# Block products for the MLP's first matrix, with weight sums added in a DRAM scratch

## The chip, the cores and the metric

The kernel runs on one core of a Trainium2 chip. The metric is the device time of one execution in microseconds. The core has five engines that run side by side, each through its own list of instructions in order: PE (matrix products, with a weight load for each), DVE and ACT (element by element), POOL (the slower general engine) and SP (which issues transfers). SP, ACT and POOL can issue transfers; 16 DMA engines carry them. An instruction waits on semaphores that other engines or finished transfers raise, and while it waits, everything behind it on its engine waits too.

## The reference

Two layers over one sequence of 512 tokens and 1024 features, in float32. Each layer is a mixer (attention and mLSTM) and an MLP:

```
def hybrid_layer(x, ...):
    h = rmsnorm(x, norm_mix)
    z = h @ w_in                      # 1024 x 4360: q, k, v, mLSTM q, k, v, gates
    ... att = sliding_window_attention(q_a, k_a, v_a, att_sinks)
    ... hm = mlstm_chunkwise(q_m, k_m, v_m, i_pre, f_pre)
    mixed = sigmoid(g_a) * (att @ w_att_branch) + sigmoid(g_m) * (hm @ w_m_branch)
    x = x + mixed @ w_out
    u = relu(rmsnorm(x, norm_ffn) @ w_ff1)      # 1024 x 4096
    return x + (u * u) @ w_ff2                  # 4096 x 1024
```

The attention looks at its own block of 128 queries and the block before it (window 128).

## The kernel before, in words

**Precision.** Every large product is made of three: each operand is split into a high part in the matrix unit's fast format (ACT copies it, `wh`, `uh`, `i`) and the rest (DVE subtracts, `wl`, `ul`, `i`), and `mm3` (L207) issues high x high, high x low and low x high into the same PSUM bank. One matmul has a 128x128 stationary block and up to 512 moving columns. So each weight element is loaded by SP, split by ACT and DVE, and used by PE.

**The mixer** (`mixer`, L359) computes the projections in groups of 12 matmuls per loaded 128x512 block of weights (`chunk`, L164: three raw buffers and four split ones). `weave` (L251) lays the dense groups out as steps of a quarter unit each and drops side work between them at given places: the attention's transposes, scores, softmax and outputs, and the mLSTM. POOL has small parts of that side work: the squares of q for its norm (L466) and of k (L469), the rotary products (L492 to L497), and the masks of the attention's probabilities (L593, L595: two for the block's own keys and two for the block before, per block b of queries and kv head, from the second block on). The attention's output matmuls (L45, `aux<-t,v`) need those masked tiles, and the branch product `att @ w_att_branch` (`mm<-a,wh`) needs the outputs.

**The MLP** (`mlp`, L802) goes through the 4096 hidden units in four parts of 1024. The first matrix is done plainly (`First`, L853): per part four groups of 256 units, each 8 x 2 x 3 = 48 matmuls of 512 columns (the 512 tokens move). Its result is scaled by the token's norm along the columns (`rowf`, made by `along`, L310), made non-negative and squared. The second matrix is done per part as one step of a 2x2 block product with seven block products in place of eight (Strassen in Winograd's form; `slots_of`, L925): the halves of the tokens and of the part's hidden units on one side, the halves of the hidden units and of the 1024 output columns on the other. Each block product has two half slots of 12 matmuls of 512 columns. The sums of weight blocks that it needs are made by DVE in SBUF (`w_minus`, L829, 128x1024, eight per part), those of the hidden units too (`u_op`, L833). The first matrix's slots of the next part stand between the second's slots of this part, and a half slot's weights are split up to five half slots ahead (`prepare`).

**What sets the order.** The program is written as Python code, and a scheduler then orders the instructions of each engine: each goes to the earliest place at which its model of the chip has the operands and the engine ready, in order of priority (what is written earlier, or under `high_priority`, first). An instruction without operands that are still being made can so move far ahead of the place where it was written. Transfers are told apart by 8 completion semaphores for those of SP and ACT (DMAHW0 to 7) and 8 for those of POOL (DMASW0 to 7), used in turn; a transfer waits at its issue until the one before it on its semaphore is complete.

The seven products' order in the kernel before, as its code has it:

```
            p1 = product("x", True, w1, lambda: a11, [(0, 0, False)])
            p5 = product("y", True, w5, s1, [(1, 1, False)])
            ...
            f = [first_slot(part + 1, q, nxt) for q in range(4)]
            return [p1, f[0], p5, p6, f[1], p3, p7, f[2], p2, f[3], p4]
```

## Time and profile before

| | |
|---|---|
| time, median of 3 runs | 1337.35 us (1336.09 to 1338.18) |
| the profiled execution, first to last instruction | 1335.6 us |
| instructions | 16885 |
| layer 0: mixer, then MLP (by the trace's stages) | 0 to 340 us, 340 to 662 us |
| layer 1: mixer, then MLP | 662 to 1000 us, 1000 to 1335 us |
| PE, DVE, ACT, POOL busy | 98%, 69%, 50%, 8% |
| bytes moved by DMA | 125.02 MB, mean 94 GB/s |

The profile gives no time for the profiled execution beside its span; the median of the runs lies 1.75 us above that span. Each engine's busy time is a share of the whole span, so an engine can be the limit in one stage and idle in another: the stages are read with the table of windows. A busy PE says that matmuls follow each other, not how fast: they overlap, so what one costs is the distance between starts, not the "mean ns" of its row. The chain that ended last tells which engine was waited for, at each place, by the work that set the end.

### The profile page before, as it was taken

To read this page: it belongs to the slowest core of one execution; us is meant where nothing else is said; L and a number is where in the kernel's file an instruction comes from. 1 tells how busy PE (TensorE), PEld (TensorE's weight loads), DVE (VectorE), ACT (ScalarE), POOL (GpSimd) and SP (SyncE) were. 2 spreads that over 40 slices of the span, in tenths; PEclk is the share of its full clock that TensorE was granted. 3 is DMA by queue.
4 is the path that set the end of the run, shared out by engine and by line. 5 is a ranking of instruction groups with operands and counts; after the bars stand their busy time and mean duration, and the time that the engine had idled before them with its cause. 6 is when DMAs were issued, how large, how long until landed. Compare 5 with 4: busy or idle time off the path is not lost.

```text
span 1335.6 us, 16885 instructions
## 1 busy us (share of the span) xinstructions
PE 1312.4 (98%) x6106; PEld 1078.1 (81%) x6106; DVE 926.3 (69%) x1409; ACT 666.4 (50%) x1201; POOL 106.7 (8%) x215
## 2 busy tenths in 40 slices
PE   8999999999999999999999999999999999999998
PEld 6877788888788888888888777888887888888886
DVE  4688764474576876868947887554646778678687
ACT  5458765544334344343554687554434444344343
POOL 4512310000000000000015013000000000000000
PEclk9999999999999999999999999999999999999999
DMA  5322122421523133131024221243216242322211
GB/s 151 108 72 72 56 79 74 140 95 64 189 95 126 63 127 125 64 119 46 34 65 123 67 71 64 72 122 96 99 54 207 73 132 81 125 95 95 95 48 63
DMA packets 87282, 125.02 MB, mean 94 GB/s; under 512 B 8216, under 2 KB 45184, under 8 KB 87200
## 3 DMA queue, kind: packets, MB, share of 16 engines
q1 hardware_dynamic: 86240, 123.30, 29.3%
q8 instruction: 48, 0.79, 0.2%
q10 hardware_dynamic: 576, 0.53, 0.1%
q0 software_dynamic: 384, 0.13, 0.1%
q14 instruction: 34, 0.28, 0.1%
HBM read 121.84 MB, written 2.10 MB: 93 GB/s over the span
## 4 chain that ended last, share of the span: by engine, by line
PE 88%; DVE 6%; ACT 4%; issue 1%; DMA 1%; POOL 0%; ACTq 0%; SPq 0%; DVEq 0%; POOLq 0%
PE mm L45 82%; PE aux L45 4%; PE aux L49 2%; ACT t L574 1%; DVE wl L191 1%; ACT wh L190 1%; DVE t L561 1%; DVE t L611 0%; DMA w<-in_w_in_dram 0%; DVE t L201 0%; ACT wh L825 0%; DVE t L538 0%; ACT junk L287 0%; DVE t L579 0%; DMA grow<-in_norm_mix_dram 0%
## 5 line engine op out<-in xcount | busy, mean ns | idle before, releaser
L45 PE MATMUL mm<-i,wh 128*128 128x512 f32 x1664 | 522.6, 393 | 2.1 <-DVE a L661 1.2
L45 PEld LDWEIGHTS mm<-i,wh 128*128 128x128 f32 x1664 | 307.7, 188 | 65.8 <-DVE a L661 2.0
L45 PE MATMUL mm<-i,wl 128*128 128x512 f32 x832 | 324.8, 390 | 0.0
L191 DVE TENSOR_TENSOR wl<-w,wh 128x512 fp32r<-128x512 f32 (+1 forms) x208 | 140.4, 677 | 131.7 <-ACT wh L190 126.8
L190 ACT ACTIVATE wh<-w 128x512 fp32r<-128x512 f32 (+1 forms) x208 | 127.2, 612 | 146.9 <-PE mm L45 123.8
L825 ACT ACTIVATE wh<-raw 128x1024 fp32r<-128x1024 f32 x112 | 118.3, 1056 | 151.9 <-PE mm L45 116.4
L45 PEld LDWEIGHTS mm<-i,wl 128*128 128x128 f32 x832 | 156.2, 188 | 33.0 <-issue 0.5
L45 PE MATMUL mm<-wh,uh 128*128 128x512 f32 x448 | 174.5, 389 | 0.0
L45 PE MATMUL mm<-wh,ul 128*128 128x512 f32 x448 | 174.3, 389 | 0.0
L45 PE MATMUL mm<-wl,uh 128*128 128x512 f32 x448 | 174.3, 389 | 0.0
L826 DVE TENSOR_TENSOR wl<-raw,wh 128x1024 fp32r<-128x1024 f32 x112 | 135.9, 1219 | 37.8 <-ACT wh L825 37.4
L45 PE MATMUL mm<-wh,i 128*128 128x512 f32 (+1 forms) x512 | 149.8, 371 | 0.4 <-ACT wh L190 0.4
L825 ACT ACTIVATE wh<-f 128x1024 fp32r<-128x1024 f32 x64 | 67.2, 1056 | 118.8 <-PE mm L45 92.3
L45 PEld LDWEIGHTS mm<-wh,i 128*128 128x128 f32 x512 | 92.7, 189 | 15.9 <-ACT wh L190 0.8
L826 DVE TENSOR_TENSOR wl<-f,wh 128x1024 fp32r<-128x1024 f32 x64 | 77.7, 1221 | 30.3 <-ACT wh L825 30.1
L45 PEld LDWEIGHTS mm<-wh,ul 128*128 128x128 f32 x448 | 84.1, 188 | 17.5
L45 PEld LDWEIGHTS mm<-wh,uh 128*128 128x128 f32 x448 | 84.1, 188 | 17.4
L45 PEld LDWEIGHTS mm<-wl,uh 128*128 128x128 f32 x448 | 84.1, 188 | 17.3
L45 PE MATMUL mm<-wl,i 128*128 128x512 f32 (+1 forms) x256 | 94.7, 370 | 0.0
L879 DVE SCALAR_TENSOR_TENSOR u<-mm,t 128x1024 f32<-128x1024 f32 x32 | 39.1, 1222 | 69.2 <-PE mm L45 69.1
L849 DVE TENSOR_TENSOR x<-x,mm 128x1024 f32<-128x1024 f32 x64 | 77.2, 1217 | 13.6 <-PE mm L45 13.6
L45 PE MATMUL mm<-wh,a 128*128 128x512 f32 x256 | 81.4, 393 | 0.0
(214 smaller groups left out, 1619.0 us busy)
## 6 DMA issues: line engine op xcount, KB each, us to landing
w<-in_w_in_dram SPq DMA_DIRECT2D x128, 256.0 KB, 2.6
f<-in_w_ff_dram SPq DMA_DIRECT2D x64, 512.0 KB, 3.7
raw<-in_w_ff_dram SPq DMA_DIRECT2D x64, 512.0 KB, 3.5
w<-in_w_out_dram SPq DMA_DIRECT2D x32, 256.0 KB, 2.5
w<-in_w_att_branch_dram SPq DMA_DIRECT2D x16, 256.0 KB, 2.5
w<-in_w_m_branch_dram SPq DMA_DIRECT2D x16, 256.0 KB, 2.5
w<-in_w_in_dram SPq DMA_DIRECT2D x16, 128.0 KB, 2.1
out_dram<-x SPq DMA_DIRECT2D x8, 256.0 KB, 2.2
```

What stands on the lines that cost most here:

```text
L45: return nc.tensor.matmul(*args, **kw)
L49: return nc.tensor.transpose(*args)
L190: sc.activation(wh[:, :off], raw[:, :off], AF.Copy)
L191: ve.tensor_tensor(wl[:, :off], raw[:, :off], f32(wh[:, :off]), op=ALU.subtract)
L561: ve.copy_predicated(dst, tri_i.unsqueeze(1).to_broadcast([P, 2, P]), p4[:, :, 1, :])
L574: sc.activation(s3[:, i, :], s3[:, i, :], AF.Exp, bias=m[:, i:i + 1], accum_out=den[:, i:i + 1])
L825: sc.activation(hi, r, AF.Copy)
L826: ve.tensor_tensor(lo, r, f32(hi), op=ALU.subtract)
L849: ve.tensor_tensor(xh, xh, ps, op=ALU.add)
L879: ve.scalar_tensor_tensor(dst, self.ps, 0.0, rowf[0].unsqueeze(1).to_broadcast([P, 2, T]), op0=ALU.max, op1=ALU.mult)
```

## The change

The first matrix, too, becomes a 2x2 block product with seven products, from the second part on (the first part stays plain). One step now takes 256 hidden units of each half of w_ff1's 4096 columns, both halves of the 1024 input features, and both halves of the tokens. The moving operand is a block of 256 tokens, so that a matmul has 256 columns; a block product has 2 x 4 x 3 = 24 of them, and a part has 2 x 7 block products (`first`). The sums of activation blocks are made once per layer from the normed activations (`left_blocks`: 8 sums and 4 splits of 128x1024). A part now consists of 512 hidden units of each half, so the second matrix's blocks are taken from the two halves of its rows (`w2_rows`).

The norm's factor is left out of the first matrix and put into the second's result instead: since the hidden units are squared, the output is scaled by the factor's square, which needs no root (`inverse`, and `gain` with a scalar per token, on two halves of 128x512). `along` is gone from the MLP.

The weight sums come from a DRAM scratch: four sums (A, D, B, C; B needs D, C needs B) of w_ff1's blocks without its first 512 columns of each half (512 rows by 1536 columns each) and four of the last part's blocks of w_ff2 (512 by 512). `sum_steps` puts them into the mixer's side work: a copy of one block from DRAM to DRAM, issued by ACT, and then a transfer issued by POOL that adds another block to it in DRAM. w_ff1's sums are cut into four groups of 128 rows (each sum 128x1536, 786 KB), w_ff2's into two of 256 rows (256x512, 524 KB): 24 copies and 24 adds per layer, 48 and 48 in all, 33.6 MB of each kind. For the other parts of w_ff2 DVE still makes the sums in SBUF, by a form of the product without negations in the weights, while the last part has none.

Buffers: a half slot's weights are split up to four ahead (`SPL = 4`), three raw buffers for w_ff1, one per kind for w_ff2; the activations are one large tile.

The core of the diff:

```diff
@@ Norm
+        def inverse(self):
+
+            v = sm([P, NB], "nv")
+            ve.tensor_tensor(v, self.ss[:, :, 0], self.ss[:, :, 1], op=ALU.add)
+            ve.tensor_scalar(v, v, 1.0 / D, EPS, op0=ALU.mult, op1=ALU.add)
+            self.inv = sm([P, 2, NB], "ninv", 2)
+            ve.reciprocal(self.inv[:, 0, :], v)
+            ve.tensor_scalar(self.inv[:, 1, :], self.inv[:, 0, :], -1.0, None, op0=ALU.mult)
...
+    SUMS = {"A": ((0, 0), (0, 1)), "D": ((0, 1), (1, 1)), "B": ((0, 0), "D"), "C": ((1, 0), "B")}
+    CUT = DFF // 2 - T
...
+            def copy(n):
+                nc.scalar.dma_start(rows(n), given(SUMS[n][0]))
+
+            def add(n):
+                nc.gpsimd.dma_start(rows(n), given(SUMS[n][1]), accum_op=ALU.add, max_dma_last_dim=4 * wide)
+
+            for d, f, names in ((0, copy, "AD"), (2, copy, "BC"), (4, add, "DA"), (8, add, "B"), (12, add, "C")):
+                steps.extend((at + d, lambda f=f, n=n: f(n)) for n in names)
+
+        for q in range(4):
+            plan(1, P, CUT, (q, lambda k, n, q=q: w1_rows(l, k, n, q)), 2.0 + 9 * q)
+        for h in range(2):
+            plan(2, 2 * P, T, (h, lambda i, j, h=h: w2_rows(l, 3, i, j, h)), 38.0 + 9 * h)
+        return steps
...
         side += [(57.75 + 1.25 * f, lambda f=f: head_tr(f)) for f in range(MH)]
+        side += sum_steps(l, sums)
...
         def gain(t, j, ps, sign, done=False):
...
-                ve.tensor_tensor(xh, xh, ps, op=ALU.add)
+                for i in range(2):
+                    b = 2 * t + i
+                    ve.scalar_tensor_tensor(xh[:, i, :], ps[:, i, :], norm.inv[:, 0 if sign > 0 else 1, b:b + 1], xh[:, i, :],
+                                            op0=ALU.mult, op1=ALU.add)
...
+        def first(part, i, u):
...
+            def weights(which):
+                at = {1: (0, 0), 3: (1, 1), 2: (1, 0)}.get(which)
+                if at:
+                    k, n = at
+                    return load1(w_ff1[l, T * k:T * (k + 1), DFF // 2 * n + c0:DFF // 2 * n + c0 + H])
+                return load1(sums[1, {5: "A", 6: "B", 7: "D", 4: "C"}[which]][:, c0 - T:c0 - T + H])
...
+            def finish(t, n, b):
+                z = to(t, n)
+                ve.tensor_tensor(z, z, of(b), op=ALU.add)
+                sc.activation(z, z, AF.Relu, scale=-1.0 if n else 1.0)
+                sc.activation(z, z, AF.Square)
...
+                    for m in range(2):
+                        c = slice(m * P, (m + 1) * P)
+                        for kt in range(4):
+                            mm3(ps[bank][:, H * m:H * (m + 1)], hi[:, kt, c], lo[:, kt, c], ah[:, kt, :], al[:, kt, :],
+                                fresh and m + kt == 0, False, skip_group_check=True)
...
+            for s, n in zip(two, (2, 2, 2, 2, 3, 3, 0)):
+                slots += [s] + nxt[:n]
+                nxt = nxt[n:]
```

How the change moves instructions. First POOL in layer 0's mixer, from the end of its setup to the first squares of q; `sum1D` and the like are the scratch sums of w_ff1, `t<-a` a square, and behind `waits` stand the semaphores (DMASW: a transfer of POOL's, DMAHW: one of SP's or ACT's). Before:

```order
L351 MEMSET sel 128x512
L156 TENSOR_SCALAR gc_103<-gc_103 128x2 [waits DMASW7_49,DMASW0_49]
L357 MEMSET cm_161 128x512
L353 AFFINE_SELECT sel<-ones 4x512 [waits Pool_49] x2
L466 TENSOR_TENSOR t_591<-a_178 128x512 [waits Activation_49,Pool_49]
```

And with the change:

```order
L429 AFFINE_SELECT sel_175<-ones 4x512 [waits Pool_49] x2
L403 DMA sum1D_615<-in_w_ff_dram 128x1536 [waits DMAHW4_49,DMASW4_49]
L403 DMA sum1A_614<-in_w_ff_dram 128x1536 [waits DMAHW0_49,DMASW5_49]
L403 DMA sum1B_616<-sum1D_615 128x1536 [waits DMAHW6_49,DMASW6_49,DMASW4_49]
L403 DMA sum1A_614<-in_w_ff_dram 128x1536 [waits DMAHW3_49]
L403 DMA sum1C_617<-sum1B_616 128x1536 [waits DMAHW0_49,DMASW6_49]
L403 DMA sum1D_615<-in_w_ff_dram 128x1536 [waits DMAHW6_49,DMASW1_49]
L403 DMA sum1B_616<-sum1D_615 128x1536 [waits DMAHW7_49,DMASW2_49,DMASW1_49]
L403 DMA sum1C_617<-sum1B_616 128x1536 [waits DMAHW3_49,DMASW3_49,DMASW2_49]
L403 DMA sum1A_614<-in_w_ff_dram 128x1536 [waits DMAHW5_49]
L403 DMA sum1D_615<-in_w_ff_dram 128x1536 [waits DMAHW0_49,DMASW5_49]
L530 TENSOR_TENSOR t_582<-a_181 128x512 [waits Activation_49,Pool_49]
```

Ten adds now stand ahead of the first square, and each B and C waits for an add that POOL issued before it.

The second place is POOL at the first masks of the attention (`t<-t`, AFFINE_SELECT), still in layer 0's mixer. Before:

```order
L639 MEMSET a_1176 64x512 [waits Pool_49]
L593 AFFINE_SELECT t_1232<-t_1228 128x512 [waits DVE_49,Activation_49,Pool_49]
L637 CAST a_1173<-a_1173 64x512 [waits Activation_49,Pool_49]
L595 AFFINE_SELECT t_1228<-t_1228 128x512 [waits DVE_49,Pool_49]
L593 AFFINE_SELECT t_1233<-t_1229 128x512 [waits PE_49]
```

With the change (the numbers 6905 to 6908 are the sums of the second layer):

```order
L704 MEMSET a_1290 64x512
L403 DMA sum1B_6907<-sum1D_6906 128x1536 [waits DMAHW5_49,DMASW5_49]
L403 DMA sum1C_6908<-sum1B_6907 128x1536 [waits DMAHW7_49,DMASW7_49,DMASW6_49]
L403 DMA sum1A_6905<-in_w_ff_dram 128x1536 [waits DMAHW2_49,DMASW0_49]
L403 DMA sum1D_6906<-in_w_ff_dram 128x1536 [waits DMAHW3_49]
L403 DMA sum1B_6907<-sum1D_6906 128x1536 [waits DMAHW2_49,DMASW1_49]
L403 DMA sum1C_6908<-sum1B_6907 128x1536 [waits DMAHW5_49,DMASW3_49,DMASW2_49]
L403 DMA sum1A_6905<-in_w_ff_dram 128x1536 [waits DMAHW7_49,DMASW4_49]
L658 AFFINE_SELECT t_1236<-t_1232 128x512 [waits PE_49,DVE_49,Activation_49,Pool_49]
L660 AFFINE_SELECT t_1232<-t_1232 128x512 [waits DVE_49,Pool_49]
```

By the first mask POOL has issued 33 adds: all 24 of layer 0 and nine of layer 1. The other 15 stand between the masks that follow and ahead of the mLSTM's masks; layer 1's own mixer has none. ACT's 48 copies stand in layer 0's mixer as well, the first three ahead of its first compute instruction.

The third place is PE at the attention's outputs (`aux<-t,v`), where `mm<-wh,i` is dense work of the mixer. Before, one such group of four:

```order
L45 MATMUL mm_1779<-wh_1920,i_315 128x512
L45 MATMUL aux_1727<-t_1646,v_115_617 128x512
L45 MATMUL aux_1727<-t_1647,v_115_617 128x512
L45 MATMUL aux_1727<-t_1650,v_115_617 128x512
L45 MATMUL aux_1727<-t_1651,v_115_617 128x512
L45 MATMUL mm_1779<-wh_1920,i_314 128x512
L45 MATMUL mm_1779<-wl_1921,i_314 128x512
```

With the change:

```order
L47 MATMUL mm_1821<-wh_1968,i_143 128x512
L51 MATMUL aux_1354<-ident,t_1118 128x128 x4
L51 MATMUL aux_1372<-ident,kvi_185 128x128
L47 MATMUL aux_1385<-t_1232,v_103_608 128x512
L47 MATMUL aux_1385<-t_1233,v_103_608 128x512
L47 MATMUL aux_1385<-t_1236,v_103_608 128x512
L47 MATMUL aux_1385<-t_1237,v_103_608 128x512
L47 MATMUL aux_1423<-kT_607,t_1113 128x256 x4
L47 MATMUL aux_1452<-kT_607,t_1333 128x256 x4
L51 MATMUL aux_1468<-ident,t_1219 128x128 x4
```

All six masked groups of layer 0's outputs now follow each other without dense work between them, behind the projections and ahead of the branch product.

423 lines of the change are left out of this document (259 added, 164 removed).

## The prediction

> **What bounds the kernel now.** I read the page's first part, then the chain that ended last, then windows by stage.
>
> ```profile
> PE 1312.4 (98%) x6106; PEld 1078.1 (81%) x6106; DVE 926.3 (69%) x1409; ACT 666.4 (50%) x1201; POOL 106.7 (8%) x215
> ...
> PE 88%; DVE 6%; ACT 4%; issue 1%; DMA 1%; POOL 0%; ACTq 0%; SPq 0%; DVEq 0%; POOLq 0%
> ...
> 365.21 296.79 PE mm L45 x1308
> ...
> core 0: us, PE busy (x) PEld busy (x) DVE busy (x) ACT busy (x) POOL busy (x), PEclk, DMA share, GB/s
> ...
> 0.00:45.00 45.00, 39.22 (x209) 32.98 (x210) 19.88 (x43) 22.97 (x49) 18.97 (x39) 1.00 0.48 134
> 45.00:110.00 65.00, 62.16 (x315) 49.54 (x314) 51.42 (x129) 37.68 (x103) 21.71 (x47) 1.00 0.30 85
> 110.00:165.00 55.00, 52.70 (x248) 40.91 (x248) 44.96 (x106) 43.89 (x109) 14.92 (x24) 1.00 0.23 68
> 362.00:662.00 300.00, 299.96 (x1325) 248.09 (x1324) 234.52 (x202) 129.57 (x125) 0.00 (x0) 1.00 0.27 89
> ```
>
> PE sets the end almost everywhere. In the first MLP the chain is one unbroken run of 1308 matmuls in 296.79 us, 0.2269 us each at 512 columns; DVE is busy for 234.52 of 300 us beside it. In layer 0's mixer PE is as full, and the DMA engines are less than half busy. So a gain must come out of PE's matmuls, and a loss from whatever makes PE wait. The change does something to each: it shortens the MLP's products and puts 67 MB of transfers, and waits on them, into the first mixer.
>
> **The MLP's products.** Plainly, three parts of the first matrix are 576 matmuls of 512 columns per layer; the block products are 3 x 14 x 24 = 1008 of 256 columns. What does half the width cost? Three places of the trace:
>
> ```profile
> 36.30 0.28 PE L45 MATMUL mm<-wl,i 128*128 128x264 f32 x1
> ...
> 45.30 0.28 PE L45 MATMUL mm<-wl,i 128*128 128x264 f32 x1
> ...
> 144.01 0.63 PE L45 MATMUL aux<-kT,t 128*128 128x256 f32 x4
> 144.48 0.39 PE L45 MATMUL mm<-wh,i 128*128 128x512 f32 x1
> ...
> L45 PEld LDWEIGHTS mm<-wh,i 128*128 128x128 f32 x512 | 92.7, 189 | 15.9 <-ACT wh L190 0.8 <-issue 0.7
> ```
>
> Between the first two starts lie 25 groups of three matmuls, 9.00 us / 75 = 0.120 us at 264 columns; four of 256 take 0.47 us, 0.1175 each. A weight load's row says 189 ns, but the loads overlap, since 264-column matmuls with a load each follow every 0.120 us. So 576 x 0.2269 = 130.7 becomes 1008 x 0.1175 = 118.4: 12.3 us per layer, with 264 scaled (0.1164) 13.4. I take 12.5, **-25 us** in both layers. Were the 189 ns a floor after all, 1008 x 0.189 = 190.5 would make it +120 in both; the 0.120 speaks against it.
>
> The vanished `along` takes two matmuls out of each MLP:
>
> ```profile
> 359.52 1.10 PE L45 MATMUL aux<-t,ones 128*128 128x512 f32 x2 [0.20 <-DVE t L315]
> ```
>
> That is **-2 us** together. The squares' root and the rows around it ran beside PE.
>
> **DVE and ACT in the MLP.** Per part, PE now has 14 half slots of the second matrix (12 x 0.2269 = 2.72) and 14 block products of the first (24 x 0.1175 = 2.82): 77.6 us. DVE's pieces:
>
> ```profile
> L826 DVE TENSOR_TENSOR wl<-raw,wh 128x1024 fp32r<-128x1024 f32 x112 | 135.9, 1219 | 37.8 <-ACT wh L825 37.4
> L826 DVE TENSOR_TENSOR wl<-f,wh 128x1024 fp32r<-128x1024 f32 x64 | 77.7, 1221 | 30.3 <-ACT wh L825 30.1
> L799 DVE TENSOR_TENSOR x<-x,mm 128x512 f32<-128x512 f32 x16 | 10.5, 684 | 16.6 <-PE mm L45 16.4
> ...
> 1300.00:1310.00 10.00, 10.00 (x46) 8.29 (x45) 10.00 (x10) 5.79 (x6) 0.00 (x0) 1.00 0.00 0
> ```
>
> 28 weight splits, 8 weight sums, 7 splits and 4 sums of hidden units are 47 x 1.22 = 57.3; 16 gains and 8 evacuations of 512 are 24 x 0.684 = 16.4: 73.7 of 77.6 us, 95%, where the window above showed 78%. It fits, with little to spare; the first part has 12 more pieces (14.6 us) beside plain slots that leave room, and the last part lost its 8 sums. Bounds: nothing, if the splits stay ahead; at most the 68 us that DVE waited for ACT's halves before, of which PE covers some 2 x 3 x 3.9 = 23: +45. In the window at 1300 us DVE is full and PE does not wait for it, so I stay near the low end: **+5 us**. The MLP's loads grow from 64 to 88 of 512 KB per layer, 46 MB in some 315 us, 146 GB/s; the MLP's window has 89 at a DMA share of 0.27, so that is less than half of the engines.
>
> **The sums in the mixer.** The copies and adds of both layers stand in layer 0's mixer, and POOL's own work stands between the adds. In the trace of before that work sits here:
>
> ```profile
> 35.48 4.22 POOL L466 TENSOR_TENSOR t<-a 128x512 f32<-128x512 f32 x4 [16.49 <-ACT a L378]
> ...
> 105.55 0.64 POOL L593 TENSOR_SCALAR_AFFINE_SELECT t<-t 128x512 fp32r<-128x512 f32 x1 [30.58 <-ACT t L200]
> ...
> 161.97 0.64 POOL L595 TENSOR_SCALAR_AFFINE_SELECT t<-t 128x512 fp32r<-128x512 f32 x1
> ...
> 162.66 0.96 PE L45 MATMUL aux<-t,v 128*128 128x512 f32 x3
> ```
>
> POOL can mask the first probabilities only when 33 adds have been issued, and the last ones after 47, where B waits for D's landing and C for B's. Those masks end at 162.6 us, and the last attention outputs start right behind them. With the change these outputs stand in PE's list after all projections, with the branch product behind: nothing dense is left to cover a late mask. So a late add delays PE one for one, from 162.6 on.
>
> How late? Up to 165 us the mixer itself moves 134 x 45 + 85 x 65 + 68 x 55 GB/s·us = 15.3 MB. The copies add 33.6 MB, the adds 33.6 MB written. The rate:
>
> ```profile
> 346.00:349.00 3.00, 3.00 (x17) 2.50 (x16) 0.12 (x1) 1.21 (x2) 0.00 (x0) 1.00 1.07 385
> ...
> w<-in_w_in_dram SPq DMA_DIRECT2D x128, 256.0 KB, 2.6
> f<-in_w_ff_dram SPq DMA_DIRECT2D x64, 512.0 KB, 3.7
> L138 POOL DMA_DIRECT2D sinks<-in_att_sinks_dram x1 | 0.5, 547 | 0.0
> ```
>
> 385 GB/s is the most that any window I read shows, at a full DMA share. No transfer from DRAM to DRAM and no add is in this trace. Low bound: an add costs what a copy costs, and both run at 385: 82.5 MB / 385 GB/s = 214 us, +52 over 162.6. Next: an add must fetch both terms, so it counts twice: 116.1 / 385 = 302 us, +139. High: DRAM serves both sides, so that reads and writes share the 385: copies 67.2, adds 100.8, loads 15.3 = 183.3 MB, 476 us, +314. I take the middle one, because an add has two operands whatever else holds, while that the two sides share a rate is not in the trace. To it comes the wait between dependent adds: from the two landings a transfer costs 1.1 us per 256 KB and about 1.5 fixed; 24 dependent waits are 36 us, and I take half, since copies and loads fill the others: +18. **+157 us** in sum. Issuing (48 x 0.55 = 26 us on POOL, as much taken for ACT) lies inside those waits. The copies also share SP's eight semaphores and the DMA engines: a weight load queued eight transfers behind a copy cannot be issued before the copy lands, with the loads behind it, and the first three copies stand ahead of ACT's first split. That makes the projections late too, but PE catches it up where it would stand still for the masks anyway. If the cover were there after all, that is if adds were free, the masks would still follow one another without dense work: six groups with four masks of 0.64 us, 15 us of POOL alone, so even then PE loses some 10.
>
> The Trainium skill, "DMA: Bandwidth & Descriptors" (section "Issuing engines are not separate DMA queues"), has transfers from all three issuing engines interleave on the same 16 DMA engines; by that the loads gain nothing from queues of their own, as my sum has it; the trace of before, with nearly all transfers from SP, can't show it. In the same page, section "Latency and other measured facts", copies between HBM tensors reach 207 to 214 GB/s per direction; by it copies and adds alone would be 67.2 MB / 214 = 314 us, near the middle case, and with adds fetched twice 471, near the high one. No row here shows it.
>
> **Sum.** 1335.6 - 25 - 2 + 5 + 157 = 1470.6; the median lies 1.75 above the profiled span: **1472 us**.
>
> **The rivals.** *DRAM to DRAM at half rate.* The high bound with the dependent waits: 1335.6 - 22 + 314 + 18 + 1.75 = 1647. For it: each byte crosses DRAM's port twice. Against: an engine that writes one packet can fetch the next. It meets the forecast at about 1550. Chance 0.25.
>
> *Cheap adds.* An add costs what a copy costs and the DMA engines never idle: 1335.6 - 22 + 52 + 1.75 = 1367. For it: the second term may be fetched while the first is under way. Against: it is a fetch more. Chance 0.19.
>
> *The adds are not the limit (the other side).* If POOL comes through its adds by 162.6 us, the MLP's gain remains, less the 0 to 10 us of the uncovered masks: 1337 - 22 + 0 to 10, 1315 to 1325. The place is the masks, the point from which it decides is 22 us of delay there: less and the change gains, more and it loses. That takes 82.5 MB in 185 us, 446 GB/s with cheap adds; against it, 385 is the highest row. Chance 0.08, with no change counted in.
>
> *Weight loads bound the narrow matmuls.* +120 in place of -25 on top of the forecast, 1617; against it stands the 0.120 us. Chance 0.03.
>
> **How the numbers follow.** Forecast (1400 to 1550) 0.45, half rate 0.25, cheap adds 0.19, narrow matmuls 0.03, not slower 0.08. The range reaches from the cheap adds' low side, 1350, to near the half rate's time, 1630. Chances, with 0.2% (2.7 us) as what this kernel's measurement can tell from no change: faster 0.06, same 0.02, slower 0.92.
>
> **What would show it.** In the changed kernel's windows, layer 0's mixer should last 480 to 500 us in place of 340, layer 1's about as before; POOL's first mask should start near 220 to 250 us and the last near 320; DMA share near 1 for the first 250 us; PE's longest waits should be at `aux<-t,v` for POOL's masks. Each MLP should take 10 to 14 us less than its 322 and 335, with narrow matmuls 0.117 us apart. Wrong it would be if POOL's waits for its adds are short or the masks lie before 180 us, if an add of 786 KB lands within 4 us under this load, or if PE waits in the MLP for DVE's `wl`.

## The result, and the profile after

The changed kernel took 1527.22 us (median; 1526.87 to 1527.76) against 1337.61 us for the kernel before: a ratio of 1.142, 95% interval 1.1406 to 1.1433, 190 us slower. The forecast was 1472 with a range of 1350 to 1630. The sign and the place were as forecast, and the mechanism in the main; two of the terms were not, and one of these is the reason why the change could not have paid even with free sums. All times are medians of fast executions: a slow one of the run "Nothing behind the adds" (2624 us) and one of the last experiment (1596 us) are left out.

The page of the changed kernel: engines, DMA queues (packets, MB, the time of their packets as a share of 16 engines' span), and the chain of waits by engine.

```profile
span 1526.0 us, 19137 instructions
...
PE 1337.5 (88%) x6966; PEld 1128.9 (74%) x6966; DVE 968.7 (63%) x1505; ACT 768.0 (50%) x1367; POOL 144.4 (9%) x267
...
q1 hardware_dynamic: 108512, 148.47, 32.4%
q0 software_dynamic: 9344, 33.69, 12.4%
q10 hardware_dynamic: 9536, 34.09, 6.4%
...
PE 72%; DMA 15%; DVE 5%; issue 4%; ACT 2%; POOL 1%; SPq 0%; ACTq 0%; DVEq 0%; POOLq 0%
```

PE fell from 98% to 88%, and 15% of the chain is now DMA, where it was 1%. The first queue carries the loads, q0 POOL's adds, q10 ACT's copies. Where did the time go? The table of windows, cut at the last write of `x` in each stage (layer 0's mixer and MLP, layer 1's mixer and MLP), of the kernel before and then of the changed one:

```profile
0.00:340.50 340.50, 329.00 (x1602) 268.59 (x1602) 211.93 (x482) 193.84 (x457) 60.76 (x125) 1.00 0.30 90
340.50:673.40 332.90, 332.54 (x1475) 274.62 (x1476) 256.82 (x234) 146.97 (x160) 0.00 (x0) 1.00 0.31 101
673.40:1000.60 327.20, 321.59 (x1578) 263.45 (x1576) 205.80 (x470) 185.89 (x440) 45.99 (x90) 1.00 0.27 82
1000.60:1335.60 335.00, 329.27 (x1452) 271.46 (x1452) 251.80 (x226) 139.71 (x144) 0.00 (x0) 1.00 0.31 102
```

```profile
0.00:526.50 526.50, 362.41 (x1602) 291.66 (x1602) 214.96 (x483) 190.45 (x454) 95.48 (x173) 0.82 0.75 191
526.50:859.80 333.30, 326.44 (x1904) 287.25 (x1904) 273.03 (x277) 198.89 (x242) 2.27 (x4) 0.99 0.42 126
859.80:1190.70 330.90, 324.51 (x1578) 265.67 (x1578) 210.55 (x475) 185.07 (x441) 46.67 (x90) 0.99 0.32 94
1190.70:1526.00 335.30, 324.13 (x1882) 284.30 (x1882) 270.14 (x273) 193.54 (x230) 0.00 (x0) 0.99 0.43 131
```

Layer 0's mixer went from 340.5 to 526.5 us: 186.0 of the 190.4. Layer 1's mixer is 3.7 us longer, and the two MLPs, whose products the change shortens, are 0.4 and 0.3 us longer. In that first mixer the same 1602 matmuls kept PE busy for 362.41 us in place of 329.00, at a granted clock of 0.82 in place of 1.00: so 153 us of the loss is PE standing still, and 33 us is PE being busy for longer. The lower clock makes nearly all of the 33: busy time times the missing share of the clock, summed over windows of 1.7 us, is 32 us (an estimate).

POOL's list in the stretch that decides, with DVE and PE where they wait for it (start, duration, instruction, and in brackets the idle time before it and what ended it):

```profile
189.28 0.56 POOL L623 MEMSET t<- 128x256 f32 x2
...
250.67 0.64 POOL L658 TENSOR_SCALAR_AFFINE_SELECT t<-t 128x512 fp32r<-128x512 f32 x1 [4.12 <-ACT t L202]
...
303.79 0.82 POOL L403 DMA_DIRECT2D sum1B<-sum1D  x1 [19.69 <-DMA sum1D<-in_w_ff_dram]
...
348.61 1.53 POOL L660 TENSOR_SCALAR_AFFINE_SELECT t<-t 128x512 fp32r<-128x512 f32 x2
```

```profile
189.62 0.45 DVE L626 COPY_PREDICATED t<-tri_l,aux 128x256 f32<-128x256 int32 x1 [32.71 <-POOL t L623]
...
190.21 0.45 PE L51 MATMUL aux<-ident,kvi 128*128 128x128 f32 x1 [36.33 <-DVE t L626]
```

And the windows up to the end of the last mask and from there to the mixer's end:

```profile
0.00:350.10 350.10, 186.45 (x773) 145.40 (x773) 117.93 (x276) 106.79 (x264) 89.16 (x156) 0.74 0.94 235
350.10:526.50 176.40, 175.97 (x830) 146.26 (x829) 97.03 (x207) 83.66 (x190) 6.33 (x18) 0.99 0.36 105
```

The first mask starts at 250.67 us (105.55 before) and the last ends at 350.1 (162.6 before): 187.5 us late, for a mixer that is 186.0 us longer. After the last mask PE is full again. Up to it PE has done 773 matmuls in 186 busy us, while the DMA engines are busy at 0.94. The longest single wait, 36.33 us, is one step ahead of the masks: a fill of -1e30 on POOL (L623), which stood behind adds and which DVE and then PE waited for.

Not all of the delay comes from the masks' place behind the adds. The first mask waited last for its own operand (ACT's split, L202), 4.12 us after POOL's add before it. By then, at 250 us, PE had done 637 matmuls, which it had done by 136 us in the run without sums (below): some 114 of the 187 us had built up ahead of the masks, by POOL's earlier work (the fill above) and by late loads, for which ACT waited 94.2 us in this mixer (`wh` for `w<-in_w_in_dram`).

### The profile page after: what moved, and what is told of

Read it like the earlier page. It is cut to its first block, busy times and chain, and to the rows that moved or that the text cites. A ratio compares the mean times of both kernels' runs of the same rounds, so it can differ in the third digit from the quotient of the medians.

```text
span 1526.0 us, 19137 instructions
## 1 busy us (share of the span) xinstructions
PE 1337.5 (88%) x6966; PEld 1128.9 (74%) x6966; DVE 968.7 (63%) x1505; ACT 768.0 (50%) x1367; POOL 144.4 (9%) x267
## 3 DMA queue, kind: packets, MB, share of 16 engines
q1 hardware_dynamic: 108512, 148.47, 32.4%
q0 software_dynamic: 9344, 33.69, 12.4%
q10 hardware_dynamic: 9536, 34.09, 6.4%
HBM read 214.11 MB, written 69.21 MB: 186 GB/s over the span
## 4 chain that ended last, share of the span: by engine, by line
PE 72%; DMA 15%; DVE 5%; issue 4%; ACT 2%; POOL 1%; SPq 0%; ACTq 0%; DVEq 0%; POOLq 0%
PE mm L47 63%; PE aux L47 8%; DMA w<-in_w_in_dram 6%; DMA sum1D<-in_w_ff_dram 4%; PE aux L51 2%; DMA sum2D<-in_w_ff_dram 1%; DMA sum1B<-sum1D 1%; DMA sum2B<-sum2D 1%; DVE wl L193 1%; ACT wh L192 1%; DMA w<-in_w_att_branch_dram 1%; DVE wl L888 0%; ACT t L639 0%; ACT wh L887 0%; DVE t L626 0%
## 5 line engine op out<-in xcount | busy, mean ns | idle before, releaser
L47 PE MATMUL mm<-i,wh 128*128 128x512 f32 (+1 forms) x1280 | 361.1, 369 | 8.4 <-ACT wh L192 8.4
L887 ACT ACTIVATE wh<-raw 128x1024 fp32r<-128x1024 f32 x212 | 223.3, 1056 | 184.2 <-PE mm L47 157.6
L888 DVE TENSOR_TENSOR wl<-raw,wh 128x1024 fp32r<-128x1024 f32 x212 | 257.4, 1220 | 67.1 <-ACT wh L887 66.6
L47 PEld LDWEIGHTS mm<-i,wh 128*128 128x128 f32 x1280 | 231.2, 194 | 44.2 <-ACT wh L192 9.5
L47 PE MATMUL mm<-i,wl 128*128 128x512 f32 (+1 forms) x640 | 234.0, 366 | 0.0
L47 PEld LDWEIGHTS mm<-i,wl 128*128 128x128 f32 x640 | 123.6, 193 | 19.6 <-DVE wl L888 0.6
L47 PE MATMUL mm<-hs,wh 128*128 128x256 f32 x576 | 106.4, 285 | 1.2 <-ACT u L1086 1.2
L47 PEld LDWEIGHTS mm<-hs,wh 128*128 128x128 f32 x576 | 90.5, 191 | 8.2 <-ACT u L1086 6.5
L934 DVE SCALAR_TENSOR_TENSOR x<-mm,ninv,x 128x512 f32<-128x512 f32 x112 | 80.3, 745 | 17.7 <-PE mm L47 17.7
L47 PE MATMUL mm<-hs,wl 128*128 128x256 f32 x288 | 81.4, 282 | 0.0
## 6 DMA issues: line engine op xcount, KB each, us to landing
sum1D<-in_w_ff_dram POOLq DMA_DIRECT2D x8, 768.0 KB, 13.8
```

The lines of the kernel that those rows point to most:

```text
L47: return nc.tensor.matmul(*args, **kw)
L887: sc.activation(hi, src, AF.Copy)
L888: ve.tensor_tensor(lo, src, f32(hi), op=ALU.subtract)
L934: ve.scalar_tensor_tensor(xh[:, i, :], ps[:, i, :], norm.inv[:, 0 if sign > 0 else 1, b:b + 1], xh[:, i, :], op0=ALU.mult, op1=ALU.add)
```

## The experiments

The question is split in two: what do the sums cost in the mixer, and why did the MLP not gain? `no_sums` answers both at once. Each time stands against that of the kernel before on the same chip.

**Without copies and adds.**

```diff
-        side += sum_steps(l, sums)
-                return load1(sums[1, {5: "A", 6: "B", 7: "D", 4: "C"}[which]][:, c0 - T:c0 - T + H])
+                return load1(w_ff1[l, 0:T, c0:c0 + H])
-                         sums[2, {5: "A", 6: "B", 7: "D", 4: "C"}[which]][H * h:H * (h + 1), :])
+                         block(0, 1, h))
```

> The changed kernel without its 48 copies and 48 adds; where it loaded a weight sum it loads a plain block of the same shape, so the sums are left out of the result. The rest is the changed kernel. Theory (the DMA engines set the loss: by the queue table of the changed kernel its adds keep all 16 engines busy for 12.4% of 1526 = 189 us and its copies for 6.4% = 98 us, next to some 50 us of loads, 337 of the 350 us to the last mask): layer 0's mixer is back at 335 to 345 us and the masks end near 163 us. The MLPs: the changed kernel's second layer took 670.0 us in place of 672.6, so its block products saved little, and the whole comes to 1330 to 1336 us. The prediction's own step for the MLP (-22 us) gives 1315. Rival (the order of PE's list costs by itself, whatever the sums do): layer 0's mixer stays 10 us or more over 340 and the whole over 1345.

Measured: 1339.4 us, ratio 1.0012 (1.0002 to 1.0021). Its windows, cut in the same way:

```profile
0.00:339.35 339.35, 328.39 (x1602) 268.39 (x1602) 214.34 (x483) 191.12 (x454) 61.81 (x125) 1.00 0.34 99
339.35:672.95 333.60, 326.72 (x1904) 287.09 (x1904) 272.96 (x276) 198.93 (x242) 2.26 (x4) 0.99 0.42 126
...
1002.20:1337.30 335.10, 323.86 (x1882) 284.95 (x1882) 270.29 (x273) 193.60 (x230) 0.00 (x0) 0.99 0.43 131
```

The mixer is back at 339.35 us, as the theory had it (its whole, 1330 to 1336, is passed by 3 us), and the attention's outputs stand in PE's list nearly where they stood before: so the 188 us between this run and the changed kernel are the copies and adds, with the order that they bring. What that order costs by itself this run does not tell; the run with copies alone does in part. And the block products by themselves bring nothing: PE is busy for 5.8 and 5.4 us less in the two MLPs (326.72 against 332.54, 323.86 against 329.27), and its idle time grew by as much (6.9 against 0.4 us, 11.2 against 5.7). The prediction's -22 us is refuted.

**Adds turned into copies.** The theory and two rivals differ by what an add costs the DMA engines.

```diff
-                nc.gpsimd.dma_start(rows(n), given(SUMS[n][1]), accum_op=ALU.add, max_dma_last_dim=4 * wide)
+                nc.gpsimd.dma_start(rows(n), given(SUMS[n][1]))
```

> The changed kernel with each add on POOL turned into a plain copy of the same block to the same place, in the same list order and with the same dependent waits; the additions are left out of the result. Theory (DMA engines, an add fetches both terms): the second queue's 189 us of all engines fall to the 98 us of a copy, the last mask comes near 260 us in place of 350, and the time is 1430 to 1445 us. Rival (POOL's dependent waits, a fixed landing each): the time stays at 1500 to 1530. Rival (DRAM's port, reads and writes sharing one rate): an add then moves three blocks' worth and a copy two, so the 189 falls to 126, last mask near 287, 1460 to 1470.

Measured: 1463.2 us, ratio 1.0938 (1.0911 to 1.0964); the theory's 1430 to 1445 is missed by 18 us. The page's queues, and the window up to the end of the last mask:

```profile
q10 hardware_dynamic: 9536, 34.09, 7.3%
q0 software_dynamic: 4608, 33.69, 7.0%
```

```profile
0.00:283.70 283.70, 177.65 (x773) 139.70 (x773) 117.50 (x276) 106.74 (x264) 74.28 (x156) 0.78 0.90 290
```

POOL's queue now keeps the engines busy for 7.0% of 1458.5 = 102 us, where its adds took 12.4% of 1526 = 189; the copies on ACT's queue took 98 there and 106 here. So an add of the same bytes costs 1.9 copies, whatever the packets' size (4608 packets here, 9344 there, and ACT's 9536 as cheap as these 4608). The last mask ends at 283.7 us in place of 350.1, 66 earlier, and the time fell by 64. Not all of the 87 us of engine time came back: the share of busy engines fell to 0.90, and POOL's dependent waits are still in its list. The time lies on the number of the rival of a shared port, but its reason does not: that one wanted 126 us on POOL's queue, and the queue shows 102.

**Copies alone.**

```diff
-            for d, f, names in ((0, copy, "AD"), (2, copy, "BC"), (4, add, "DA"), (8, add, "B"), (12, add, "C")):
+            for d, f, names in ((0, copy, "AD"), (2, copy, "BC")):
```

> The changed kernel with its 48 copies where they stand, and without the 48 adds; the additions are left out of the result. It tells what the copies alone cost. POOL's list has nothing new in it. If the bytes matter: 34 MB of copies at the 349 GB/s that their queue's time gives are 98 us of all engines, with 20 us of loads ahead of 45 us; PE's first products come late and the mixer is 25 to 60 us longer, 1365 to 1400 us in all. If only POOL's waits matter: 1338 to 1348.

Measured: 1384.9 us, ratio 1.0357 (1.0337 to 1.0378), as the first case of the expectation. The bytes matter even where POOL waits for none of them: the last mask ends at 210.2 us, mostly since loads and with them the projections came late.

```profile
0.00:210.20 210.20, 170.88 (x773) 136.33 (x773) 118.64 (x274) 106.37 (x263) 54.41 (x109) 0.89 0.76 235
```

But 14 of these 46 us are lost in one place, and there the order of PE's list is the likely reason. This run has the changed order too, in which the last masked groups follow each other without dense work between them. The stretch up to the last masked outputs, about as many matmuls, in this run and then in the run without sums:

```profile
183.60:211.00 27.40, 16.96 (x57) 12.23 (x57) 17.43 (x45) 15.70 (x53) 10.05 (x17) 0.60 0.59 184
```

```profile
152.40:165.70 13.30, 12.99 (x58) 9.59 (x57) 9.97 (x29) 9.50 (x30) 5.57 (x8) 1.00 0.20 61
```

So the 188 us come as 46 for the copies with their order (1339.4 to 1384.9), 78 for a second set of copies behind which POOL's list waits (to 1463.2), and 64 for what an add costs the engines beyond a copy (to 1527.2). Taken away in another order, the parts could have other sizes.

**No add waits for another sum.**

```diff
-    SUMS = {"A": ((0, 0), (0, 1)), "D": ((0, 1), (1, 1)), "B": ((0, 0), "D"), "C": ((1, 0), "B")}
+    SUMS = {"A": ((0, 0), (0, 1)), "D": ((0, 1), (1, 1)), "B": ((0, 0), (1, 0)), "C": ((1, 0), (1, 1))}
```

> The changed kernel with B and C adding a plain block of the weights in place of the sum D or B, so that no add has to wait for another sum; the bytes and the numbers of copies and adds are the same, and these parts of two sums are left out of the result. Theory (DMA engines are full at a share of 0.95 for the first 300 us): only the order changes, 1510 to 1527 us. The prediction's term for the dependent waits, 18 us, gives 1509. Rival (POOL's dependent waits set the pace): the waits of B's and C's adds, 74.7 + 32.6 + 49.9 + 39.7 + 14.7 = 212 us in the table of waits, go, and the time falls by 100 us or more, to 1430 or less.

Measured: 1501.6 us, ratio 1.1225 (1.1203 to 1.1247): 26 us less than the changed kernel, where the prediction's term said 18 and the rival more than 100. The window to the last mask says why:

```profile
0.00:329.30 329.30, 191.96 (x773) 149.64 (x773) 118.54 (x276) 107.25 (x264) 92.55 (x157) 0.77 0.98 248
```

The share went from 0.94 to 0.98 and the same bytes were through 21 us earlier. The waits between adds only cost where they leave the engines idle.

**Each layer's sums in its own mixer.**

```diff
+                with tc.issue_after(last_split[0].ins):
                     nc.scalar.dma_start(rows(n), given(SUMS[n][0]))
+                pace[0] = gp.tensor_copy(pt, f32(last_hi[0][0:1, 0:1]))
+                with tc.issue_after(pace[0].ins):
                     nc.gpsimd.dma_start(rows(n), given(SUMS[n][1]), accum_op=ALU.add, max_dma_last_dim=4 * wide)
```

> The changed kernel with each copy held behind ACT's latest split and each add behind a one-element copy on POOL that reads that split, so that a layer's sums stay in that layer's mixer; nothing is left out. Theory (DMA engines): each mixer then has half of the transfers, 144 us of all engines' time beside its own 0.30 x 340 = 102, 246 of 340 us, which fits; what is left is the masks that stand behind the first adds on POOL. 1345 to 1385 us, with layer 0's mixer at 350 to 370 and layer 1's 345 to 360. Rival (POOL's list: 24 dependent waits per layer that cost a landing each, whatever the load): the landings are shorter but the waits are as many, so both mixers lose about 90 us and the time stays at 1500 to 1530.

Measured: 1488.1 us, ratio 1.1124 (1.1102 to 1.1146). My theory failed here by over 100 us, and the rival (1500 to 1530, about 90 per mixer) was nearer: both mixers lost 74 us, with the engines partly idle. The attention's masks were done at 186.7 us, but now the mLSTM's masks (L788 here) stood behind adds. The windows of the two mixers, and one such place in the timelines of POOL and PE:

```profile
0.00:413.80 413.80, 348.93 (x1603) 282.51 (x1603) 216.42 (x483) 191.22 (x454) 83.77 (x173) 0.91 0.61 162
747.00:1150.00 403.00, 341.43 (x1574) 275.85 (x1574) 210.82 (x473) 185.33 (x441) 69.47 (x138) 0.91 0.61 159
```

```profile
204.51 0.83 POOL L410 DMA_DIRECT2D sum1B<-sum1D  x1 [16.09 <-DMA sum1D<-in_w_ff_dram]
...
218.61 0.80 PE L47 MATMUL aux<-a,a 128*128 128x256 f32 x2 [18.45 <-DVE t L794]
```

PE waited 39.2 us in the first mixer, and 80.3 us in all, for tiles of DVE's (L794) behind these masks. So half the bytes per mixer, at a mean share of 0.61, cost as much as 74 us, and more than half of it is a wait in an engine's list with other work behind it.

**Nothing behind the adds.** All 24 adds of a layer stand behind that mixer's last mask, and each four places from the one that it needs.

```diff
+                with tc.issue_after(last_mask[0].ins):
                     nc.gpsimd.dma_start(rows(n), given(SUMS[n][1]), accum_op=ALU.add, max_dma_last_dim=4 * wide)
+            steps.extend((200.0 + 10 * m + "DABC".index(n), lambda n=n: add(n)) for n in "DABC")
+            last_mask[0] = gp.affine_select(out=e[:, 0:P], ...
```

> The changed kernel with each copy held behind ACT's latest split and all 24 adds of a layer held behind that mixer's last mask on POOL, ordered D, A, B, C with the four groups of each side by side, so that no add stands right behind the one it needs; nothing is left out. In the run with the sums held in their mixers the DMA engines were not full (shares of 0.3 to 0.9) and PE waited 80.3 us for mLSTM tiles whose masks stand behind adds on POOL. Theory now (POOL's list: an add that waits for a landing holds the masks behind it, and that, not the bytes, is most of the loss): with nothing behind the adds 1338 to 1352 us, masks at their old times (110 and 161 us), both mixers 338 to 345. Rival (bytes: copies, adds and loads share the engines, so loads come late wherever the transfers stand): each mixer or MLP 15 us or more longer, 1370 or more. Rival (sums late for the MLP): PE waits in each MLP for weights whose sum has not landed, 1355 to 1370.

Measured: 1432.0 us, ratio 1.0705 (1.0678 to 1.0733). The rival that counts bytes holds here: no mask stood behind an add (the last ended at 175.6 us, against 161.6 without sums), but each mixer was still 46 to 47 us longer than without sums (last writes of `x` at 385.4, 718.7 and 1095.3 us). In layer 0, 13 us of this had built up before the first add, with the copies: PE had done 991 matmuls at 221 us, which it had done at 208 without sums. The other 33 came with the adds. The window of the adds in layer 0, and the landing times of the weight blocks issued in it:

```profile
222.00:325.00 103.00, 86.69 (x383) 69.58 (x381) 36.17 (x74) 35.40 (x65) 19.67 (x24) 0.92 1.05 240
```

```profile
DMA to landing us min/median/max: 7.2/11.8/18.8
```

While the 24 adds run, the engines are full, and a weight block of 256 KB, here 24 of them, lands 11.8 us after its issue. Without sums the same loads land after 2.7 us in the median. Waits for masks had been traded for waits for weights.

**One at a time.** Copies and adds spread over layer 0's mixer and MLP and layer 1's mixer, an add every 10 or 11 us.

```diff
+            side += [(2.0 + 1.5 * i, f) for i, f in enumerate(copies[:16])]
+            side += [(40.0 + 3.0 * i, f) for i, f in enumerate(copies[16:])]
+            side += [(10.0 + 3.5 * i, f) for i, f in enumerate(adds[:16])]
...
+            if i % 4 == 1 and l == 0:
+                k = i // 4
+                cs, ads = tosum[1][0][:16], tosum[0][1][16:] + tosum[1][1][:16]
```

> The changed kernel with its 48 copies and 48 adds spread one by one: layer 0's first-matrix sums over layer 0's mixer, an add every 3.5 dense steps (about 10 us), its last-part sums and layer 1's first-matrix sums over layer 0's MLP (one every four half slots, 11 us), layer 1's last-part sums over layer 1's mixer; each copy is held behind ACT's split of a weight and each add behind a one-element copy on POOL that reads that split, and each add stands four or more adds behind the one it needs. Nothing is left out. With all 24 adds of a layer in a row behind the masks the time was 1433 us: the engines were full (share 1.05 for 103 us) and loads of 256 KB took about 12 us, though no mask waited. Theory (what costs is the bunching: an add keeps all 16 engines for some 4 us, and loads behind several of them come late; POOL's waits were the other half): one add at a time stays inside what the loads are issued ahead, 1338 to 1350 us, near the 1339.4 without any sums. Rival (an add delays loads one for one wherever it stands: 48 x 3.9 + copies, of which loads lose what they overlap): 1360 to 1400. Rival (the sums land too late for the MLP's first block products): PE waits at raw blocks of sums, 1350 to 1365.

Measured: 1381.9 us, ratio 1.0325 (1.0303 to 1.0347), the best version with real sums, but inside the first rival's range and not the theory's: 42 us over the run without sums. The stages:

```profile
0.00:371.10 371.10, 340.98 (x1602) 278.12 (x1602) 218.03 (x483) 191.26 (x454) 78.00 (x157) 0.95 0.61 169
371.10:715.60 344.50, 329.58 (x1904) 288.87 (x1904) 273.02 (x276) 199.06 (x242) 48.85 (x52) 0.99 0.74 207
715.60:1043.60 328.00, 321.17 (x1567) 262.93 (x1568) 210.23 (x472) 184.92 (x441) 56.56 (x106) 1.00 0.45 120
```

Layer 0's mixer, with 16 adds and 24 copies, is 32 us longer than without; the MLP with 24 adds and 16 copies 11; layer 1's mixer with 8 adds and 8 copies not at all. So spreading returns 145 of the 188 us. What is left is not set by the bytes alone: the first two stretches have the same, 29.4 MB of copies and adds each, and lose 32 and 11 us. In the mixer the masked groups without dense work between them again stand at the end of the attention. Whether another order or a slower pace there would hide the rest was not tried; by the next runs it would not have made the kernel faster than before.

**Why the MLP did not gain.** In the changed kernel a group of 24 narrow matmuls and one of 24 wide ones take this by the chain of waits:

```profile
606.55 2.88 PE aux L47 x24
609.43 5.47 PE mm L47 x24
```

In the parts with narrow matmuls, three per layer, PE waits at places like these (timeline of PE):

```profile
664.67 0.47 PE L47 MATMUL mm<-wh,uh 128*128 128x512 f32 x1 [0.78 <-DVE x L934]
665.46 0.50 PE L47 MATMUL mm<-hs,wh 128*128 128x256 f32 x2 [0.32 <-ACT u L1086]
...
711.43 0.50 PE L47 MATMUL mm<-wl,uh 128*128 128x512 f32 x1 [0.67 <-DVE wl L888]
...
746.99 0.50 PE L47 MATMUL mm<-hs,wh 128*128 128x256 f32 x2 [0.32 <-ACT u L1086]
```

A narrow matmul takes 2.88 / 24 = 0.120 us. From 665.46 to 746.99 lies one part, 81.5 us. Its matmuls are 168 x 0.2267 + 336 x 0.120 = 78.4 us; before, 360 x 0.2269 = 81.7. So 3.3 us were saved, and 3.1 us of distance between starts are waits for a bank that DVE (and ACT) had not yet read and for a split that came late. Not every part has all of these waits: from 583.04 to 829.44 us, as many matmuls as three parts have, 528 wide and 984 narrow ones take 246.4 us where their prices give 237.8, so the waits are 8.6 us per layer. Five runs, all on the kernel without sums, were to tell whether these waits come from DVE's load or from the buffers.

The sums on POOL (and likewise the other three):

```diff
-                    plus(b11[h], b11[h], b12[h])
+                    plus(b11[h], b11[h], b12[h], gp)
```

> The kernel without copies and adds (plain blocks loaded in place of sums) with the second matrix's eight weight sums per part on POOL in place of DVE: 8 x 1.22 = 9.8 us of each part's 81.5 leave DVE; by POOL's 128x512 product row (4.03 us for four) one of 128x1024 takes about 2 us there, 16 us of 81.5. The sums of the first matrix and of the last part are left out. Theory (DVE's queue makes the splits late): the 3 us of waits per part shrink to 1 or less, 1326 to 1333 us. Rival (the buffers or the order of PE's list make the waits): 1336 to 1342. Rival (POOL slows DVE down while both run): DVE's rows get longer and the time goes over 1342.

Measured: 1359.9 us, ratio 1.0167 (1.0152 to 1.0183). The third case of the expectation: DVE's splits became longer for it. The row of the groups by form in the run without sums, then two rows of this run:

```profile
L887 DVE TENSOR_TENSOR wl<-raw,wh 128x1024 fp32r<-128x1024 f32 x212 | 257.2, 1219 | 67.2 <-ACT wh L886 66.7
```

```profile
L887 DVE TENSOR_TENSOR wl<-raw,wh 128x1024 fp32r<-128x1024 f32 x212 | 300.8, 1429 | 73.9 <-ACT wh L886 73.4
...
L901 POOL TENSOR_TENSOR raw<-raw,raw 128x1024 f32<-128x1024 f32 x48 | 133.2, 2778 | 693.2 <-DVE wl L887 684.9 <-issue 7.3
```

The mean split went from 1219 to 1429 ns, and POOL's sum took 2778 ns where 2 us were expected. So the same sums were left out (one of the four lines):

```diff
-                    plus(b11[h], b11[h], b12[h])
```

> The kernel without copies and adds (plain blocks in place of sums), and without the second matrix's eight weight sums per part on DVE in three parts of each MLP; all sums of weights are left out. Putting these on POOL made the time longer, 1359.9 in place of 1339.4 us, with DVE's split at 1429 ns in place of 1219: the two engines slow each other, so that run could not tell whether DVE's work makes PE wait. Here 8 x 1.22 = 9.8 of DVE's 72 us per part go for nothing. Theory (DVE's queue makes the splits late): the 3 us of waits per part go, 18 us in 6 parts, 1320 to 1328 us. Rival (split buffers, banks and the order of PE's list make the waits): 1334 to 1340.

Measured: 1331.7 us, ratio 0.9957 (0.9941 to 0.9974), 7.7 us less than without sums: neither case, some 40% of the theory's 18. In its table of waits those for banks and hidden units are nearly gone and those for the low part stay:

```profile
PE mm L47 <- DVE wl L887: 4.0, 6, 0.7
PE mm L47 <- DVE x L933: 3.2, 4, 0.8
...
PE mm L47 <- DVE ul L887: 1.2, 2, 0.6
```

```profile
PE mm L47 <- DVE wl L887: 4.0, 6, 0.7
...
PE aux L51 <- DVE x L933: 0.6, 2, 0.4
```

(the run without sums, then this one; the numbers are the sum in us, the count and the longest wait). So these sums on DVE make the waits for `x` and `ul`, though DVE is busy for only 85% of a part (window below); the six waits for `wl` stay without them.

The buffers, in the kernel that still makes these sums:

```diff
-SPL = 4
+SPL = 5
-        raws = pool(phase, "raws", 3)
+        raws = pool(phase, "raws", 2)
+                return pieces(t, *(uspl.tile([P, 4, H], F32R, tag=n, name=nm(n), bufs=k) for n, k in (("uh", 2), ("ul", 1))))
```

> The kernel without copies and adds (plain blocks loaded in place of sums) with five split buffers in place of four, paid for by two raw buffers in place of three and one low part of hidden units in place of two; the sums are left out. Without sums the MLPs took 323.5 and 337 us against 322.5 and 333.5 before, though their matmuls are 9.7 us shorter per layer (1008 x 0.120 against 576 x 0.2267): about 3 us per part go into waits of PE for DVE's weight split, for a bank and for ACT. Theory (split buffers: four free them too late): the waits shrink, 1322 to 1331 us. Rival (DVE and ACT have no room, whatever the buffers): 1336 to 1343. Rival (the buffers taken away cost more): over 1345.

Measured: 1363.8 us, ratio 1.0199 (1.0184 to 1.0214): the buffers taken away cost more. PE waited 17.9 us for `ul`. Without that cut:

```diff
+                return pieces(r, *(spl.tile(list(r.shape), F32R, tag=t, name=nm(t), bufs=k) for t, k in (("wh", 5), ("wl", 4))))
-            prepare(i + SPL)
+            prepare(i + 5)
-        raws = pool(phase, "raws", 3)
+        raws = pool(phase, "raws", 2)
```

> The kernel without copies and adds (plain blocks in place of sums) with five buffers for the high parts of the MLP's weights, four as before for the low parts, splits issued five half slots ahead, and two raw buffers in place of three; the sums are left out. In the run with five of both, one buffer for the low part of the hidden units was taken away too, and PE waited 17.9 us for just that: it could not tell. Theory (the split buffers make the rest of the waits, where PE waits 0.67 us per part for DVE's low part): ACT's half is ready when a low buffer comes free, 1330 to 1337 us. Rival (the scheduler's order and DVE's queue make them): 1337 to 1342. Rival (a raw buffer less makes loads late): 1345 or more.

Measured: 1345.7 us, ratio 1.0060 (1.0045 to 1.0075): the lower edge of the rival of the raw buffer; the waits for `wl` were 3.9 us as before, in four places, and SP waited 43.6 us at loads of raw blocks for earlier ones, 6.5 in the run without sums. With the sums of `no_plus` left out as well:

> The same with the second matrix's eight weight sums per part left out of three parts of each MLP too, against the 1331.7 us of that alone. There PE's waits for banks and hidden units had gone, and six waits of 0.67 us for DVE's low part of a weight were left, about 1 us of distance between starts each. Theory (split buffers): these go, 1322 to 1328 us. Rival (order of the lists): 1329 to 1334. Rival (a raw buffer less makes loads late): 1337 or more.

Measured: 1333.2 us, ratio 0.9965 (0.9949 to 0.9981), not to be told from the 1331.7, and in the range of the rival (order of the lists). The waits for `wl` had shrunk to 0.4 us, and others for `wh` and `ul` (2.3 and 1.6 us) stood in their place. That the split buffers cause the rest is thus neither shown nor excluded, since each buffer added had to be taken from another use: it stays open. What is shown is that with all sums of weights left out the best of these versions is 6 us below the kernel before, and not 22.

## Why the prediction was right or wrong

**MLP's products, -25: the form right, the size too high.** A narrow matmul takes 0.120 us, not 0.1175, and a part's saving is 3.3 us, 9.8 us per layer, 20 in all. The rival of weight loads as a floor (0.189 us each) is refuted by the same rows.

**How far off.** The median lies 55 us above the forecast: 29 us come from the sums in the mixer (186 for 157) and 26 from the rest (4 us more in place of 22 less). Both errors have the same sign, and the range of 280 us was wide enough for both.

**DVE and ACT in the MLP, +5: the step that failed.** It was right that it can lie between 0 and 45 and wrong to stay near the low end. Waits took 8.6 us per layer, 17 us in all. The reason given, "DVE is full and PE does not wait for it", was read from 10 us of the kernel before and its order. DVE was busy for less than was counted, 72.02 of 85 us in this window of the changed kernel, 85% and not 95%:

```profile
1260.00:1345.00 85.00, 83.24 (x528) 74.69 (x527) 72.02 (x72) 50.25 (x61) 0.00 (x0) 1.00 0.45 137
```

So DVE's throughput, which the step worked out, was not the limit. Leaving eight sums per part out of its list took the waits for banks and hidden units away and returned 7.7 us. That a bank's reading, a split and a sum stand in one list at the moment when PE needs one of them fits this but is not shown by itself, and what makes the other waits stays open. The start of the MLP costs too: behind the 1.46 us that PE waits there for the activations, a stretch of 3.7 us ran at a granted clock of 0.63 (below). So "-22 with free sums" is +1.5 us (0.3 to 2.8 by the interval), and the rival that ended on the other side, 1315 to 1325, could not have come true: there was no gain left for its deciding point to weigh.

**Sums in the mixer, +157: the mechanism right in the main, the size low by 30.** The engines were full until the last mask, the last mask came 187.5 us late and the mixer was 186.0 longer, one for one, as argued. (That alone does not prove that the masks' place in POOL's list is the reason: with copies alone, too, last mask and mixer are late by about as much, 49 and 46 us.) Of the three bounds the middle one has the right form: an add costs 1.93 copies by the queues (189 against 98 us of all engines), not one (cheap adds, 1367), and not 1.5 as in the high bound, which counts a copy twice and an add three times. With both terms counted the first 350.1 us moved 33.6 + 2 x 33.6 + 15.1 = 116 MB in 0.94 x 350.1 = 329 us of full engines, 353 GB/s where 385 was taken: the rate was the highest of a window of 3 us with loads only. That is 27 of the 30 us. *DRAM to DRAM at half rate* falls: 34.09 MB of copies took 98 us of all engines, 349 GB/s, as fast as the loads (148.47 MB in 32.4% of 1526 = 494 us, 300 GB/s). The wait between dependent adds, +18, came out at 21 to 26.

**Projections late, "but PE catches it up where it would stand still for the masks anyway": half right.** It holds for the changed kernel, where both delays end together. But it hid that late loads cost by themselves: some 32 of the 46 us with copies alone, and most of the 46 per mixer in the run with nothing behind the adds. The prediction had one mechanism, POOL's list; the runs show two of similar size, and taking one away leaves the other. The small term beside it, "even then PE loses some 10" for masked groups without dense work, was right in kind: 14 us with copies alone.

**What would show it.** First mask forecast at 220 to 250 us, found at 250.7, though its last wait was for its operand and not for an add, so that the reason given is only part of it; last near 320, found at 350.1; mixer 480 to 500, found 526.5; DMA share near 1 for 250 us, found 0.94 for 350. PE's waits at `aux<-t,v` for POOL's masks sum to 44.4 us, but the longest is elsewhere: the fill at L623 for the first block's scores is POOL work too, and the list of POOL's instructions in the prediction left it out. An add's landing, set at more than 4 us, is 9.5 (`sum1C<-sum1B`) to 13.8 us (`sum1D<-in_w_ff_dram`) in the median.

"Each MLP 10 to 14 less" was not found, and "PE waits in the MLP for DVE's `wl`", which the prediction had named as what would make it wrong, was.

## What to carry to other kernels

A transfer without operands that are still being made goes to the front of its engine's list, and an engine's list is in order: before moving work to the DMA engines, look at what stands behind each issue, then at what it does to the landing of loads that were issued just in time. Both have to be held in check, or curing one only uncovers the other. And before paying for a saving of PE, check it with its inputs for free: here one run without the sums showed that there was nothing to pay for.

## What the runs showed of the hardware that was not expected

**Waits make PE slow as well as idle.** In the changed kernel's first mixer the same 1602 matmuls took 34 us more of busy time than in the run without sums (362.41 against 328.39), at a granted clock of 0.82 in place of 1.00. It can come without a long pause: at the MLP's start in the run without sums PE was busy for 1.84 of 3.35 us, with no wait over 1.46 us, and the next 3.7 us had this clock:

```profile
339.35:342.70 3.35, 1.84 (x10) 1.37 (x11) 2.09 (x3) 2.90 (x4) 0.00 (x0) 0.90 0.00 0
342.70:346.40 3.70, 3.70 (x13) 2.95 (x12) 3.51 (x5) 3.30 (x6) 0.00 (x0) 0.63 0.48 138
```

The Trainium skill, "TensorE: Matmul & The Clock Gate" (Part 1, on the clock gate), has the throttle come back after about one idle window of 3.4 us and leave after one busy one. The length agrees with the second: if the low clock is a half, as it is from 342.70 to 344.00 us, the two windows hold 0.67 and 2.74 us of it, 3.4 us in all (an estimate). For the first, a stretch that was only about half idle sufficed, but PE's work in it was transposes only (`aux<-ident,x`, from 338.0 to 342.7 us); whether these count like dense products no run here shows.

**DRAM to DRAM is not slow, an accumulating transfer is.** With POOL's adds turned into copies, 290 GB/s were moved for 283.7 us at a share of 0.90; 67 MB of it, 237 GB/s, went from DRAM to DRAM. The Trainium skill, "DMA: Bandwidth & Descriptors" (section "Latency and other measured facts"), gives 207 to 214 GB/s per direction for copies between HBM tensors at its two best row pitches; this run is over that, so the figure is no ceiling here. The cost of an add, 1.9 copies of engine time, shows in the queue's time only: POOL's queue has 33.69 MB and DRAM 214.11 MB read with adds and with copies alike. Whether it is a second fetch is therefore not shown.

**DVE is slower beside POOL's sums.** With eight sums of 128x1024 per part on POOL, DVE's splits took 1429 in place of 1219 ns in the mean, so that moving 9.8 us of work per part off DVE left it busier: 988.0 us in place of 967.5.
